# A seventh pair by seven products, its weights streamed in a pinned order

## The chip, the cores and the metric

The kernel runs on one core of a Trainium2 chip. The metric is device time in microseconds (us) of one execution, the median over the runs of a kernel. A core has TensorE (PE in the profile; its weight loads are PEld), VectorE (DVE), ScalarE (ACT), GpSimd (POOL) and SyncE (SP), each with its own instruction queue, and 16 DMA engines that move data between the device memory (HBM, "dram" in the names) and the on-chip memory. Matmuls write accumulators called banks; the program has eight.

## The reference

Two layers of a decoder trunk on x of 512 tokens by 1024 features, in float32. Each layer is an FFN, a mixer (a gated recurrence beside a spatial gate), and another FFN, each followed by a layer norm:

```python
def swiglu(x, w13, w2):
    a, b = jnp.split(x @ w13, 2, axis=-1)
    return (jax.nn.silu(a) * b) @ w2

for l in range(DEPTH):                       # DEPTH = 2
    x = layer_norm(ALPHA * x + 0.5 * swiglu(x, ffn1_w13[l], ffn1_w2[l]), ...)
    x = layer_norm(ALPHA * x + mixer(x, ...), ...)
    x = layer_norm(ALPHA * x + 0.5 * swiglu(x, ffn2_w13[l], ffn2_w2[l]), ...)
```

So there are four FFNs. Each has a hidden width of 2816 = 22 blocks of 128; w13 holds 22 blocks for a and 22 for b. The change touches the first multiplication of each FFN (x by w13) and the first microseconds of the program; the second multiplication and the mixer are as they were.

## The kernel before

**Splitting.** Every operand of a matmul is split in two parts of a format that TensorE takes: hi, a rounded copy made by ScalarE, and lo, the rest, made by VectorE from source and hi (`split`, L117 to L122). A product then takes three matmuls, hi by hi, hi by lo and lo by hi. A weight block is fetched by SyncE's queue into a tile of the ring "raw" (four buffers), then split into two tiles of the ring "w" (ten buffers, so five weights). Other rings are "rs" (two buffers), "sa" (three) and the slots "h" (33).

**Plain blocks.** The hidden blocks are taken in eleven pairs (k, k + 11). A plain block j is `pair_of` with two calls of `proj`: 24 matmuls of 512 columns for a and 24 for b (L147), then `glu`: silu on ScalarE and a product on VectorE (L593, L594). A plain pair is two such blocks.

**Seven products.** Six of the eleven pairs are instead done as a 2 by 2 block multiplication with seven products in place of eight (`seven_pair`). The weights of a pair are four quarters: a, the upper halves of the two a blocks; c, their lower halves; b and d, the same of the two b blocks, chosen by column and row. From the quarters VectorE forms sums (t13, t2 and one more), so that there are seven weights of 128 x 1024, each split into hi and lo. The tokens' side has its own sums s1 to s4, made once per FFN (`x_sums`). Each product is 24 matmuls of 256 columns (L548) into one of the banks A, B, C, E; ScalarE and VectorE then combine the banks (L557 to L572). A, C and E are used twice in a pair: the second product adds on top of the first, so it waits until the first value has been read.

**The order within an FFN.** Three pairs in front by plain blocks (pairs 8, 9, 10), then six by seven products (0 to 5), then two behind by plain blocks (6, 7). Then `Seven.run` does the second multiplication, by the same scheme; for it `weight_sums`, `activation_sums` (for each pair, four operations and two splits on VectorE and two copies on ScalarE, L330 to L336) and `sums_in_dram` (additions done by DMAs in GpSimd's queue) prepare operands. The activation sums of nine pairs are issued between the four plain blocks behind.

**What sets the order on an engine.** The program is written as one stream, and a planner orders each engine's queue by the readiness that it computes. Side work (`Flow`) is put into the stream when a written clock passes its due time. `tc.keep_in_program_order` ties one instruction behind the instruction of the same engine that was written just before it. Before the change it is used on the rounded copies of two weights (c and d) in each pair and on the DMAs of `sums_in_dram`. On an engine, instructions start in the order of its queue.

**The weights of a pair before.** `weights_of_pair` fetches the quarters into two tiles of "raw" and two of "rs" (for the first pair into slots, two blocks ahead), splits five of the seven weights into the ring "w" and two into slots, and is issued ahead of the pair's products. The program starts with `first_block`, which puts six matmuls on a tile of zeros ahead of the first real one.

Of the kernel before, what the change touches and what calls it, by code (L numbers as in the profile page):

```python
# [40 lines left out]
NF = DFF // P  # L41
# [42 lines left out]
def trunk(ctx: ExitStack, tc, x_in, xt_in, w13, w2, w_in, w_br, w_out, ln_g, ln_b, lb_in, hgn, sgg, sgb, sgws,  # L84
          sgbs, masks, tril_in, ident_in, out):
    nc = tc.nc
    V, S, G, PE = nc.vector, nc.scalar, nc.gpsimd, nc.tensor
# [3 lines left out]
    wk = ctx.enter_context(tc.tile_pool(name="wk", bufs=1))  # L91
# [11 lines left out]
    def slot(name, dtype=F32):  # L103
        return big.tile([P, 2, 512], dtype, tag="h", name=name, bufs=NS)
# [10 lines left out]
    xh, xl = [None] * 4, [None] * 4  # L115


    def split(hi, lo, src, pinned=False):
        act = S.activation(hi, src, AF.Copy)  # L119
        if pinned:  # L120
            tc.keep_in_program_order(act)
        V.tensor_tensor(lo, src, hi.bitcast(F32), op=ALU.subtract)  # L122

    def weights(src, name, early=False):

# [10 lines left out]
    NW = 10  # L136
    NS, NRAW, NSA = 33, 4, 3
# [46 lines left out]
    H = slice(0, 512), slice(512, 1024)  # L184
# [75 lines left out]
    NH2 = NF // 2  # L260

    class Seven:
# [51 lines left out]
        def activation_sums(self, k):  # L314

            r = self.r[k]
            x = wk.tile([P, 2, 256], F32, tag="sa", name="s12", bufs=NSA)
            if k >= self.KEPT:
                hi, lo = (quads(f"t{c}{k}", F32R) for c in "hl")
                parts = hi[:, 0], lo[:, 0], hi[:, 1:3], lo[:, 1:3]  # L320
            elif self.last is None:
                hi, lo = (quads(f"t{c}{k}", F32R) for c in "hl")
                self.last = hi, lo
                parts = hi[:, 0], lo[:, 0], hi[:, 1:3], lo[:, 1:3]
            else:
# [4 lines left out]
            V.tensor_tensor(x[:, 0], r[:, 2], r[:, 3], op=ALU.subtract)  # L330
            V.tensor_tensor(x[:, 1], r[:, 0], x[:, 0], op=ALU.subtract)
            split(parts[0], parts[1], r[:, 0])
            V.tensor_tensor(r[:, 2], r[:, 0], r[:, 2], op=ALU.subtract)
            V.tensor_tensor(r[:, 0], r[:, 1], x[:, 1], op=ALU.subtract)
# [152 lines left out]
            s[c] = hi, lo  # L487
        return s

    def raw_cd(w13_of, k, early=False):  # L490

        if early:
            rc, rd = slot(f"rc{k}"), slot(f"rd{k}")
        else:
            rc, rd = (wk.tile([P, 2, 512], F32, tag="rs", name=f"r{c}{k}", bufs=2) for c in "cd")
        for z, j in enumerate((k, k + NH2)):
            nc.sync.dma_start(rd[:, z], w13_of(NF + j)[:, H[0]])
            nc.sync.dma_start(rc[:, z], w13_of(j)[:, H[1]])
        return rc, rd

    def weights_of_pair(w13_of, k, rcd=None):

        js = (k, k + NH2)
        ra = [wk.tile([P, 2, 512], F32, tag="raw", name=f"r_p{j}", bufs=NRAW) for j in js]
        rc, rd = rcd or raw_cd(w13_of, k)
        t13 = [slot(f"t13{j}") for j in js]
        t2 = slot(f"t2{k}")
        for z, j in enumerate(js):
            wa, wb = w13_of(j), w13_of(NF + j)
            nc.sync.dma_start(ra[z][:, 0], wa[:, H[0]])  # L510
            nc.sync.dma_start(ra[z][:, 1], wb[:, H[1]])

        def parts(raw, name, early=False):
            hi, lo = ((slot(f"{v}_{name}", F32R) if early else
                       wk.tile([P, 2, 512], F32R, tag="w", name=f"{v}_{name}", bufs=NW)) for v in "hl")
            split(hi, lo, raw, early)
            return [(hi[:, z], lo[:, z]) for z in range(2)]

        p = [parts(ra[z], f"p{j}") for z, j in enumerate(js)]
        for z in range(2):  # L520
            V.tensor_tensor(t13[z], ra[z], rd[:, z:z + 1].broadcast_to([P, 2, 512]), op=ALU.add)
            V.tensor_tensor(t2[:, z], ra[z][:, 0], t13[z][:, 1], op=ALU.add)  # L522
        w2 = parts(t2, f"t2{k}")
        wt = [parts(t13[z], f"t{j}") for z, j in enumerate(js)]
        w21 = parts(rc, f"c{k}", True)
        V.tensor_tensor(rc, rc, t2, op=ALU.add)
        w4 = parts(rc, f"d{k}", True)
        return p, wt, w2, w21, w4

    def seven_pair(seven, s, k, w):  # L530

        p, wt, w2, w21, w4 = w
        half = slice(0, 256), slice(256, 512)
        movs = {"A11": lambda m: (xh[m // 2][:, m % 2, half[0]], xl[m // 2][:, m % 2, half[0]]),
                "A12": lambda m: (xh[2 + m // 2][:, m % 2, half[0]], xl[2 + m // 2][:, m % 2, half[0]]),
                "A22": lambda m: (xh[2 + m // 2][:, m % 2, half[1]], xl[2 + m // 2][:, m % 2, half[1]])}
        for c in s:
            movs[c] = lambda m, c=c: (s[c][0][:, m], s[c][1][:, m])

        def product(ps, units, c, first=True):  # L540
            for z in range(2):
                hi, lo = units[z]
                for m in range(4):
                    ms = slice(m * P, (m + 1) * P)
                    mh, ml = movs[c](m)
                    for i, (a, v) in enumerate(((hi, mh), (hi, ml), (lo, mh))):
                        start = first and z == 0 and m == 0 and i == 0
                        PE.matmul(ps[:, half[z]], a[:, ms], v, start=start, stop=(m == 3 and i == 2),  # L548
                                  skip_group_check=not (first and z == 0))
# [6 lines left out]
        product(A, [p[0][0], p[1][0]], "A11")  # L556
        S.activation(upper, A, AF.Copy)  # L557
        product(B, w2, "s2")
        V.tensor_tensor(upper, upper, B, op=ALU.subtract)
        product(C, [wt[0][0], wt[1][0]], "s1")  # L560
        V.tensor_tensor(b1, C, upper, op=ALU.subtract)
        product(E, [wt[0][1], wt[1][1]], "s3")
        V.tensor_tensor(b1, b1, E, op=ALU.subtract)
        product(A, w21, "A12", False)
        S.activation(lower, A, AF.Silu)
        product(C, [p[0][1], p[1][1]], "s4", False)
        V.tensor_tensor(b0, C, upper, op=ALU.subtract)
        V.tensor_tensor(lower, lower, b0, op=ALU.mult)
        product(E, w4, "A22", False)
        V.tensor_tensor(upper, E, upper, op=ALU.add)  # L570
        S.activation(upper, upper, AF.Silu)
        V.tensor_tensor(upper, upper, b1, op=ALU.mult)  # L572

    S_PAIRS = 6

    def ffn(l, i, last=False, first_of_all=False):
        seven = Seven(lambda k: w2[l, i, k])
# [22 lines left out]
        sums = iter(range(NH2))  # L600
# [25 lines left out]
        for z, j in enumerate(js[2:]):  # L626
            args = blocks(j)
            if z == 3:
                w = weights_of_pair(w13_of, by_seven[0], rcd)
            plain(j, args)  # L630
            if z == 0:
                s = x_sums()
            if z == 1:
                rcd = raw_cd(w13_of, by_seven[0], True)
            if z == 0:
                seven.weight_sums(next(sums))
            if z == 1:
                seven.activation_sums(front[1])
        in_dram = flow.add(seven.sums_in_dram(list(sums)))
        for k in by_seven:  # L640
            seven_pair(seven, s, k, w if k == by_seven[0] else weights_of_pair(w13_of, k))
        due = [front[2:] + by_seven[:2], by_seven[2:5], by_seven[5:] + behind[:1], behind[1:]]
# [361 lines left out]
    def first_block(wa, wb):  # L1004
# [2 lines left out]
        zero = wk.tile([P, T], F32, tag="sa", name="zero", bufs=NSA)  # L1007
        V.memset(zero[:, 0:P], 0.0)
        idle = bank("idle")
        for _ in range(6):  # L1010
            PE.matmul(idle[:, 0:P], zero[:, 0:P], zero[:, 0:P], start=True, stop=True)
        rw = [wk.tile([P, D], F32, tag="raw", name=f"r_{c}0", bufs=NRAW) for c in "ab"]
        w = [[wk.tile([P, D], F32R, tag="w", name=f"{c}_{v}0", bufs=NW) for c in "hl"] for v in "ab"]
# [137 lines left out]
```

## Time and profile before

| | |
|---|---|
| median of 3 runs | 2078.19 us (2078.13 to 2081.96) |
| the profiled execution, its own time | 2075.15 us |
| its span in the profile | 2073.4 us |
| busy: TensorE, its weight loads, VectorE, ScalarE, GpSimd | 2058.6, 1814.0, 1465.6, 871.3, 284.7 us |
| stage of six pairs by seven products, second FFN | 764.1 to 885.1 us |
| four plain blocks behind it | 885.1 to 928.7 us |

Times in the profile are counted from the first instruction. A row of the timeline reads: start, duration, engine, line, operation, output and inputs by tile names, sizes, count, and in brackets the idle time of the engine ahead of it with what ended it. In rows of groups the mean duration of one is in nanoseconds. A row of DMA issues ends with the median time from issue to landing; "SPq" is SyncE's queue. The rows of waits give total, count and longest, in us.

### The profile page before, as it was taken

What the parts mean: (1) busy time and instruction counts of PE and PEld (TensorE: products, weight loads), DVE (VectorE), ACT (ScalarE), POOL (GpSimd) and SP (SyncE); (2) the same over time, 40 slices, a digit from 0 to 9 for tenths busy, and PEclk for the clock granted to TensorE, in tenths of its full rate; (3) what the DMA queues carried; (4) which work ended last, traced back from release to release, by engine and by line L of the source; (5) the groups of instructions that cost most, each with busy time, mean ns of one, the idle gap of its engine ahead of it and who ended that gap; (6) DMA issues with size and microseconds to landing.
All of it is one profiled execution on the core that took longest, in us unless ns stands there. A gap on an engine that the chain in (4) does not pass through costs nothing.

```text
span 2073.4 us, 30387 instructions
## 1 busy us (share of the span) xinstructions
PE 2058.6 (99%) x11764; PEld 1814.0 (87%) x11764; DVE 1465.6 (71%) x2285; ACT 871.3 (42%) x1219; POOL 284.7 (14%) x424
## 2 busy tenths in 40 slices
PE   9999999999999999999999999999999999999998
PEld 7999888888888989988899998888888888899886
DVE  7986878943535788777778878779444357987776
ACT  4443555234322434446534445542343224444453
POOL 1222002001000222210112220020010002122001
PEclk9999999999999999999999999999999999999999
DMA  8788677122243578867768886861222436788674
GB/s 300 226 236 205 194 267 250 42 82 82 82 156 98 205 222 218 210 172 275 238 219 244 219 216 194 275 209 52 82 90 84 143 97 237 218 217 218 178 264 141
DMA packets 142849, 381.27 MB, mean 184 GB/s; under 512 B 16624, under 2 KB 16880, under 8 KB 142704
## 3 DMA queue, kind: packets, MB, share of 16 engines
q1 hardware_dynamic: 100368, 258.13, 37.3%
q0 software_dynamic: 42336, 121.20, 22.7%
q8 instruction: 92, 1.51, 0.3%
q14 instruction: 53, 0.43, 0.1%
HBM read 344.66 MB, written 101.71 MB: 215 GB/s over the span
## 4 chain that ended last, share of the span: by engine, by line
PE 96%; DMA 2%; DVE 1%; ACT 1%; issue 0%; POOL 0%; SPq 0%; POOLq 0%; DVEq 0%; ACTq 0%
PE pa L147 9%; PE pb L147 9%; PE z L147 8%; PE fC L548 7%; PE fE L548 7%; PE fA L548 7%; PE pA L363 6%; PE pC L363 6%; PE y L229 4%; PE y L147 4%; PE fB L548 3%; PE pB L363 3%; PE pE L363 3%; PE pF L363 3%; PE q L147 2%; PE f L147 2%
## 5 line engine op out<-in xcount | busy, mean ns | idle before, releaser
L122 DVE TENSOR_TENSOR l_b<-r_b,h_b 128x1024 fp32r<-128x1024 f32 (+1 forms) x85 | 102.5, 1210 | 54.3 <-ACT h_b L119 53.8
L288 POOL DMA_DIRECT2D t<-in_w_dram x128 | 106.5, 885 | 215.5 <-DMA t<-in_w_dram 102.7
L147 PE MATMUL pa<-xh,l_a 128*128 128x512 f32 (+1 forms) x360 | 130.0, 361 | 1.0 <-DVE l_a L122 1.0
L147 PE MATMUL pa<-xl,h_a 128*128 128x512 f32 (+1 forms) x360 | 130.4, 362 | 0.5 <-DVE xl L122 0.5
L147 PE MATMUL pb<-xh,h_b 128*128 128x512 f32 (+1 forms) x360 | 130.3, 362 | 0.0
L147 PE MATMUL pa<-xh,h_a 128*128 128x512 f32 (+1 forms) x360 | 130.3, 362 | 0.0
L147 PE MATMUL pb<-xh,l_b 128*128 128x512 f32 (+1 forms) x360 | 129.9, 361 | 0.0
L147 PE MATMUL pb<-xl,h_b 128*128 128x512 f32 (+1 forms) x360 | 129.8, 361 | 0.0
L119 ACT ACTIVATE h_b<-r_b 128x1024 fp32r<-128x1024 f32 (+1 forms) x85 | 89.0, 1047 | 91.4 <-PE pa L147 34.1
L122 DVE TENSOR_TENSOR l_t<-t,h_t 128x1024 fp32r<-128x1024 f32 x72 | 87.3, 1222 | 42.1 <-ACT h_t L119 42.1
L119 ACT ACTIVATE h_t<-t 128x1024 fp32r<-128x1024 f32 x72 | 75.4, 1058 | 67.5 <-DVE t L522 49.1
L147 PE MATMUL z<-xh,h_z 128*128 128x512 f32 x256 | 102.6, 401 | 0.0
L147 PE MATMUL z<-xh,l_z 128*128 128x512 f32 x256 | 99.8, 390 | 0.0
L147 PE MATMUL z<-xl,h_z 128*128 128x512 f32 x256 | 99.8, 390 | 0.0
L122 DVE TENSOR_TENSOR l_z<-r_z,h_z 128x1024 fp32r<-128x1024 f32 x32 | 39.2, 1225 | 72.5 <-ACT h_z L119 72.4
L119 ACT ACTIVATE h_p<-r_p 128x1024 fp32r<-128x1024 f32 x48 | 50.4, 1058 | 69.5 <-PE fE L548 48.9
L147 PEld LDWEIGHTS pa<-xh,l_a 128*128 128x128 f32 x360 | 67.8, 188 | 11.7 <-DVE l_a L122 1.4
L147 PEld LDWEIGHTS pa<-xl,h_a 128*128 128x128 f32 x360 | 67.9, 189 | 11.4 <-DVE xl L122 1.2
L229 PE MATMUL y<-h_wo,yt 128*128 128x512 f32 x256 | 77.3, 392 | 0.0
L147 PEld LDWEIGHTS pa<-xh,h_a 128*128 128x128 f32 x360 | 67.9, 189 | 10.5 <-ACT xh L119 0.3
L147 PEld LDWEIGHTS pb<-xh,l_b 128*128 128x128 f32 x360 | 67.9, 189 | 10.4
L147 PEld LDWEIGHTS pb<-xl,h_b 128*128 128x128 f32 x360 | 67.9, 189 | 10.3
(363 smaller groups left out, 6704.2 us busy)
## 6 DMA issues: line engine op xcount, KB each, us to landing
t<-in_w_dram POOLq DMA_DIRECT2D x64, 512.0 KB, 9.1
r_p<-in_w_dram SPq DMA_DIRECT2D x96, 256.0 KB, 7.6
r_c<-in_w_dram SPq DMA_DIRECT2D x44, 512.0 KB, 5.8
r_d<-t SPq DMA_DIRECT2D x88, 256.0 KB, 4.2
r_a<-in_w_dram SPq DMA_DIRECT2D x39, 512.0 KB, 5.3
r_b<-in_w_dram SPq DMA_DIRECT2D x39, 512.0 KB, 5.5
t<-t POOLq DMA_DIRECT2D x76, 256.0 KB, 4.0
t<-in_w_dram POOLq DMA_DIRECT2D x64, 256.0 KB, 5.6
```

Source lines behind the costliest of these rows:

```text
L119: act = S.activation(hi, src, AF.Copy)
L122: V.tensor_tensor(lo, src, hi.bitcast(F32), op=ALU.subtract)
L147: PE.matmul(ps[:, n0:n0 + n], a[:, cs], m[:, n0:n0 + n], start=(i == 0), stop=(i == 3 * nk - 1))
L229: PE.matmul(ys[t][q], a[:, ts], m[:, q * 512:(q + 1) * 512], start=(k == 0 and i == 0), stop=(k == nk - 1 and i == 2))
L288: tc.keep_in_program_order(nc.gpsimd.dma_start(*of(k), **kw))
L363: PE.matmul(ps[tt], a[:, ts], m, start=(start and k == 0 and z == 0), stop=(stop and k == NH2 - 1 and z == 2), skip_group_check=not start)
L548: PE.matmul(ps[:, half[z]], a[:, ms], v, start=start, stop=(m == 3 and i == 2), skip_group_check=not (first and z == 0))
```

## The change

Seven pairs (0 to 6) go by seven products and one (7) stays plain behind them. A class `PairWeights` fetches the four quarters into a, b and d in the ring "raw" and c in "rs"; the sum t13's part t3 = d + b has the other buffer of "rs", and the sums b + a, a + t3 and later c + a overwrite the quarters. All seven weights of a pair are split into the ring "w". The weights of the next pair are written between the products of the running one, at fixed places, and while `pinned` is set each ScalarE and VectorE instruction of the stage is tied behind the one written before it. The activation sums of pairs 10, 0, 1 and 2 are written behind the seven-product pairs 0 to 3, in the same order; those of pairs 3 to 7 stay between the plain blocks. Ten matmuls on zeros stand ahead of the first real one.

```diff
+    pinned = [False]
+    def pin(ins):
+        if pinned[0]:
+            tc.keep_in_program_order(ins)
+    def split(hi, lo, src):
+        pin(S.activation(hi, src, AF.Copy))
+        pin(V.tensor_tensor(lo, src, hi.bitcast(F32), op=ALU.subtract))
...
+    class PairWeights:
+        def __init__(self, w13_of, k):
+            self.w13_of, self.k, self.w = w13_of, k, {}
+            self.a, self.b, self.d = (self.raw(c, "raw", NRAW) for c in "abd")
+            self.t3 = self.raw("t", "rs", 2)
+            self.load(self.a, 0, 0)
+            self.load(self.b, NF, 0)
+            self.load(self.d, NF, 1)
+        def raw(self, c, tag, n):
+            return wk.tile([P, 2, 512], F32, tag=tag, name=f"r{c}_{self.k}", bufs=n)
+        def load(self, to, col, row):
+            for z, j in enumerate((self.k, self.k + NH2)):
+                nc.sync.dma_start(to[:, z], self.w13_of(col + j)[:, H[row]])
+        def load_last(self):
+            self.c = self.raw("c", "rs", 2)
+            self.load(self.c, 0, 1)
+        def parts(self, p):
+            src = {1: "a", 6: "a", 5: "b", 7: "t3", 2: "c", 3: "d", 4: "c"}[p]
+            hi, lo = (wk.tile([P, 2, 512], F32R, tag="w", name=f"{v}_p{p}_{self.k}", bufs=NW) for v in "hl")
+            split(hi, lo, getattr(self, src))
+            self.w[p] = hi, lo
+        def sums(self):
+            for to, u, v in ((self.t3, self.d, self.b), (self.b, self.a, self.b), (self.a, self.a, self.t3)):
+                pin(V.tensor_tensor(to, u, v, op=ALU.add))
+        def last_sum(self):
+            pin(V.tensor_tensor(self.c, self.a, self.c, op=ALU.add))
...
+        pw.parts(2)
+        pw.last_sum()
+        if next_of is not None:
+            nx = next_of()
+        product(A, w[1], "A11")
+        pin(S.activation(upper, A, AF.Copy))
+        pw.parts(3)
+        product(B, w[6], "s2")
+        pin(V.tensor_tensor(upper, upper, B, op=ALU.subtract))
+        pw.parts(4)
+        if nx:
+            nx.load_last()
+        product(C, w[5], "s1")
+        pin(V.tensor_tensor(b1, C, upper, op=ALU.subtract))
+        if nx:
+            nx.parts(1)
+        product(E, w[7], "s3")
+        pin(V.tensor_tensor(b1, b1, E, op=ALU.subtract))
+        if nx:
+            nx.sums()
+            nx.parts(6)
+        product(A, w[2], "A12", False)
+        pin(S.activation(lower, A, AF.Silu))
+        if nx:
+            nx.parts(5)
+        product(C, w[3], "s4", False)
+        pin(V.tensor_tensor(b0, C, upper, op=ALU.subtract))
+        pin(V.tensor_tensor(lower, lower, b0, op=ALU.mult))
+        if nx:
+            nx.parts(7)
+        product(E, w[4], "A22", False)
+        pin(V.tensor_tensor(upper, E, upper, op=ALU.add))
+        pin(S.activation(upper, upper, AF.Silu))
+        pin(V.tensor_tensor(upper, upper, b1, op=ALU.mult))
+        for v in due:
+            seven.activation_sums(v)
+        return nx
-    S_PAIRS = 6
+    S_PAIRS = 7
...
             if z == 3:
-                w = weights_of_pair(w13_of, by_seven[0], rcd)
+                pinned[0] = True
+                pw = PairWeights(w13_of, by_seven[0])
+                pw.load_last()
+                pw.parts(1)
+                pw.sums()
+                for p in (6, 5, 7):
+                    pw.parts(p)
+                pinned[0] = False
...
+        pinned[0] = True
         for k in by_seven:
+            pw = seven_pair(seven, s, k, pw, (lambda: PairWeights(w13_of, k + 1)) if k < by_seven[-1] else None,
+                            ([front[2]], by_seven[0:1], by_seven[1:2], by_seven[2:3], [], [], [])[k])
+        pinned[0] = False
+        due = [by_seven[3:6], by_seven[6:] + behind]
...
-        for _ in range(6):
+        for _ in range(10):
             PE.matmul(idle[:, 0:P], zero[:, 0:P], zero[:, 0:P], start=True, stop=True)
```

More of the change, by code (lines that the diff above doesn't have):

```diff
@@ L115, in trunk @@
     xh, xl = [None] * 4, [None] * 4
[L118 to L122, printed above, removed]
+    pinned = [False]
[5 more added lines that the diff above has]
+        pin(V.tensor_tensor(lo, src, hi.bitcast(F32), op=ALU.subtract))
     def weights(src, name, early=False):
@@ L488, in x_sums @@
         return s
[L490 to L528, printed above, removed]
@@ L533, in seven_pair @@
+    def seven_pair(seven, s, k, pw, next_of, due):
+        w, nx = pw.w, None
         half = slice(0, 256), slice(256, 512)
@@ L541, in product @@
             for z in range(2):
-                hi, lo = units[z]
+                hi, lo = units[0][:, z], units[1][:, z]
                 for m in range(4):
@@ L555, in seven_pair @@
         b0, b1 = (wk.tile([P, T], F32, tag="sa", name=f"b{c}", bufs=NSA) for c in "01")
[L556 to L572, printed above, removed]
-    S_PAIRS = 6
+        pw.parts(2)
[36 more added lines that the diff above has]
+    S_PAIRS = 7
     def ffn(l, i, last=False, first_of_all=False):
```

14 lines of the change are left out of this document (4 added, 10 removed).

## The prediction

> **What bounds the kernel now.** I read the page's first part, then the stages in the view of stretches, then the chain of waits and who waits on TensorE, then the order of VectorE in one seven-product stage.
>
> ```profile
> span 2073.4 us, 30387 instructions
> PE 2058.6 (99%) x11764; PEld 1814.0 (87%) x11764; DVE 1465.6 (71%) x2285; ACT 871.3 (42%) x1219; POOL 284.7 (14%) x424
> ```
>
> TensorE works for 2058.6 of 2073.4 us. So either a change takes matmul time away, or it makes TensorE wait. The stretches are those of the seven-product stage and of the plain blocks behind it, in the second FFN (the others agree within 0.4 us of VectorE):
>
> ```profile
> core 0: us, PE busy (x) PEld busy (x) DVE busy (x) ACT busy (x) POOL busy (x), PEclk, DMA share, GB/s
> 764.10:885.10 121.00, 121.00 (x1010) 121.00 (x1009) 99.39 (x111) 53.72 (x60) 27.77 (x40) 1.00 0.86 217
> 885.10:928.70 43.60, 43.60 (x194) 36.07 (x193) 30.41 (x62) 17.29 (x30) 5.55 (x8) 1.00 0.62 167
> ```
>
> The stage of six pairs takes 121.0 us without a gap on TensorE, while VectorE works 99.4 us in it (16.6 a pair) and the 16 DMA engines are 0.86 busy. The four plain blocks behind it have more air on both: 30.4 of 43.6 us, and 0.62. The chain of waits in time order and TensorE's list of waits:
>
> ```profile
> 77.82 2.88 PE fB L548 x24
> 80.70 2.88 PE fC L548 x24
> ...
> 195.90 5.47 PE pa L147 x24
> 201.37 5.44 PE pb L147 x24
> ```
>
> ```profile
> PE pa L1041 <- ACT xh L119: 1.4, 1, 1.4
> PE idle L1011 <- DVE zero L1008: 1.1, 1, 1.1
> PE pa L147 <- DVE l_a L122: 1.0, 1, 1.0
> PE pb L1041 <- ACT h_b L119: 0.7, 1, 0.7
> ```
>
> A product is 24 matmuls in 2.88 us; a plain block is 5.44 + 5.44. All listed waits lie in the first 65 us. VectorE's pace inside the stage:
>
> ```profile
> 766.25 1.22 DVE L122 TENSOR_TENSOR l_c<-rc,h_c 128x1024 fp32r<-128x1024 f32 x1
> 767.51 1.22 DVE L526 TENSOR_TENSOR rc<-rc,t 128x1024 f32<-128x1024 f32 x1
> 769.86 1.23 DVE L122 TENSOR_TENSOR l_d<-rc,h_d 128x1024 fp32r<-128x1024 f32 x1 [1.12 <-ACT h_d L119]
> 771.00 0.68 DVE L559 TENSOR_TENSOR r<-r,fB 128x512 f32<-128x512 f32 x1
> 771.60 1.22 DVE L122 TENSOR_TENSOR l_p<-r_p,h_p 128x1024 fp32r<-128x1024 f32 x1
> 772.73 1.22 DVE L521 TENSOR_TENSOR t<-r_p,rd 128x1024 f32<-128x1024 f32 x1
> 773.87 0.68 DVE L561 TENSOR_TENSOR b<-fC,r 128x512 f32<-128x512 f32 x1
> ```
>
> From start to start a full operation (128x1024) takes 1.14 us and a half one (128x512) 0.60; 1.26 where the second overwrites what the first reads (766.25 to 767.51). A sum whose rounded copy is its own next operand costs VectorE 1.12 us of waiting on ScalarE. Today the stage interleaves sums and splits of several weights, and ten of the fourteen hi/lo tiles of a pair go through the w ring and four into other slots, so these waits cost TensorE nothing.
>
> **The change part by part.**
>
> *Matmuls.* One pair per FFN goes from two plain blocks, 4 x 5.44 = 21.76 us, to seven products, 7 x 2.88 = 20.16. That is 1.60 us each, 6.4 us over four FFNs.
>
> *Ten matmuls on zeros instead of six.*
>
> ```profile
> 1.07 2.93 PE L1011 MATMUL idle<-zero 128*128 128x128 f32 x12 [1.07 <-DVE zero L1008]
> 5.44 0.79 PE L1041 MATMUL pa<-xh,h_a 128*128 128x512 f32 x1 [1.44 <-ACT xh L119]
> 6.96 0.80 PE L1041 MATMUL pb<-xh,h_b 128*128 128x512 f32 x1 [0.73 <-ACT h_b L119]
> 7.55 0.63 PE L1041 MATMUL pa<-xl,h_a 128*128 128x512 f32 x1
> ...
> 9.26 0.63 PE L1041 MATMUL pa<-xh,h_a 128*128 128x512 f32 x1
> ```
>
> Six show as 12 records in 2.93 us, so four more add at most 2.0 us and end near 6.0; the second real matmul waits until 6.96 anyway. Between 7.55 and 9.26 four matmuls start 0.43 us apart, later ones 0.23 apart. The most that full speed could save on the seven matmuls from 6.96 on is 7 x 0.20 = 1.4 us; the worst is the 2.0 us of the extra zeros. Behind both stands the wait of 1.0 us on l_a that ends at 64.22, whose chain does not pass through these matmuls:
>
> ```profile
> 33.26 6.44 DMA rb_w<-in_w_dram
> ...
> 62.95 1.23 DVE l_a L122
> 64.18 0.04 issue
> 64.22 5.29 PE pa L147 x22
> ```
>
> An earlier TensorE only waits longer there. I take 0 (bounds -1.4 and +1.0, the extra zeros' 2.0 less what that wait swallows).
>
> *VectorE's work per pair.* Old: ten full operations and nine half ones. New: seven splits, three sums and the last sum, eleven full, and seven evictions, 11 x 1.14 + 7 x 0.60 = 16.7 us; the same. ScalarE keeps seven copies and three evictions, some 9 us of 20.16, and costs nothing of itself.
>
> *The activation sums moved in.* Four of nine (for the pairs front[2], 0, 1, 2) are now issued behind pairs 0 to 3, in the pinned order:
>
> ```profile
> 903.14 0.42 DVE L331 TENSOR_TENSOR s<-r,s 128x256 f32<-128x256 f32 x1
> ...
> 905.42 0.42 DVE L331 TENSOR_TENSOR s<-r,s 128x256 f32<-128x256 f32 x1
> ```
>
> Six operations from one L331 to the next, 2.28 us. With them VectorE has 19.0 us of work in 20.16. The five that stay behind fit: 5 x 2.28 + 2 x (2 x 1.14 + 0.60) = 17.2 us in the 21.76 of the two last blocks, and pair 6 has no successor, which leaves VectorE 11 us free. I cost that at nothing; without that cover it would be those 17.2 less whatever of the 21.76 is gone.
>
> *The order itself.* Every ScalarE and VectorE instruction of the stage is now tied to the one traced before it. So each wait on VectorE holds everything behind it, evictions too. I follow one pair in program order, from the eviction of its predecessor's last product (start to start; L568 to L572 stands for the round trip through Silu):
>
> ```profile
> 885.27 0.69 DVE L570 TENSOR_TENSOR r<-fE,r 128x512 f32<-128x512 f32 x1
> 886.65 0.69 DVE L572 TENSOR_TENSOR r<-r,b 128x512 f32<-128x512 f32 x1 [0.70 <-ACT r L571]
> 887.26 0.75 DVE L330 TENSOR_TENSOR s<-r 128x256 f32<-128x256 f32 x2
> ```
>
> (i) upper+E, Silu, times b1: 1.99. (ii) activation sums: 2.28. (iii) split 2, then the last sum over the operand just read, to its end: 1.26 + 1.22 = 2.48. (iv) split 3, subtract B, split 4, b1 from C, split 1 of the next pair, subtract E: 3 x 1.14 + 3 x 0.60 = 5.2. (v) three sums: 3.42. (vi) wait for the copy of the last of them 1.12, split 6 1.14. (vii) split 5 with 0.3 of waiting (ScalarE does the Silu of the fifth product, 0.6, between two copies): 1.44. (viii) b0 and its product, the second needing the first: 1.29; split 7: 1.14. Sum: 1.99 + 2.28 + 2.48 + 5.2 + 3.42 + 2.26 + 1.44 + 2.43 = **21.5 us** with activation sums, 19.2 without. TensorE's period is 20.16.
>
> *The load of the next pair.* A pair holds three raw tiles (a, b, d) of a ring of four. At the time its loads are traced, only the fourth and b's have been let go; the third must wait for the last sum of the running pair, (iii), the last reader of a. With tiles given as they come free that is d, and the first of the three sums (v) needs d. Such a load is two DMAs of 256 KB; the sync queue issues them right when the buffer is free:
>
> ```profile
> 775.07 1.22 DVE L521 TENSOR_TENSOR t<-r_p,rd 128x1024 f32<-128x1024 f32 x1
> ```
>
> ```profile
> 776.31 0.80 SPq L497 DMA_DIRECT2D rd<-in_w_dram  x2
> ```
>
> ```profile
> rd<-in_w_dram SPq DMA_DIRECT2D x48, 256.0 KB, 7.2
> rc<-in_w_dram SPq DMA_DIRECT2D x48, 256.0 KB, 6.8
> ```
>
> ```profile
> DMA to landing us min/median/max: 2.5/6.8/11.4
> ```
>
> The last row is rc's, which like the new d is issued as two alone. I take its 6.8 us (bounds 2.5 and 11.4). If (iv)'s 5.2 us are replaced by this wait, the ring last sum, d, sums, splits, evictions, last sum takes 16.3 + 6.8 = **23.1 us** with activation sums and 20.8 without. Behind the waiting sum stand the splits of parts 6, 5 and 7 and the evictions b0 and the last two; TensorE waits for all of them. Behind d's DMAs in the sync queue stand the next a and the next c, both with a pair's time to spare. POOL's queue, with its sums in DRAM, is neither passed nor moved; its traffic is what the loads share the DMA engines with.
>
> The Trainium skill (DMA: Bandwidth & Descriptors, "Anatomy of one DMA — SWDGE (gpsimd) path") gives one transfer about 2.0 us plus its bytes at 436 GB/s, fitted on the other DMA path; for 512 KB that is an estimate of 3.2 us. By it d would be in time and the sum would be that of the first rival below; the median of 6.8 us at a DMA share of 0.86 says otherwise.
>
> *What TensorE feels.*
>
> ```profile
> L548 PE MATMUL fA<-xh,h_p 128*128 128x256 f32 x192 | 54.3, 283 | 0.0
> ```
>
> A product's last matmul ends 0.16 us after its 0.12 us slot. So subtracting E in pair 0 can start at 4 x 2.88 + 0.2 = 11.7 us of the pair; (v) to (viii) follow, so the eviction at its end starts at 11.7 + 0.6 + 3.42 + 2.26 + 1.44 + 2.43 = 21.9, a lag of 1.7 over 20.16. Each pair behind activation sums (1 to 4) adds 23.1 - 20.16 = 2.9, pair 5 adds 0.6: 1.7 + 11.6 + 0.6 = 13.9 us at the end. The room: product six of a pair reuses C and must wait for b1, which ends 1.99 + 2.28 + 2.48 + 1.14 + 0.60 + 1.14 + 0.68 = 10.3 us after the late eviction began, against the sixth product's start at 14.4. Room: 4.1 us. The w ring gives the same to within 0.3: split 6 must end 23.3 us after the pair's start and ends 6.75 + 6.8 + 3.42 + 1.12 + 1.22 = 19.3 after the eviction. So TensorE loses 13.9 - 4.1 = **9.8 us** an FFN, 39 in all. The d of pair 0, whose quarters were fetched two blocks ahead before and are not now, is a further 0 to 1.8 each (its buffer comes free some 11 us ahead of the stage, its first use is 3 us into it); I take 0.
>
> *Sum.* -6.4 + 39 + 0 = +33 us on the profiled execution's 2075.15: 2108. The median of the runs shown is 3.0 over it, so **2111 us**.
>
> **Rivals.**
>
> *d lands in time.* If loads take 5.2 us or less, the loop is 21.5 and the lag grows by 1.3 in four pairs and shrinks afterwards: 1.7 + 5.4 - 4.1 = 3.0 an FFN, 12 in all, -6.4 + 12 = +5.6, so 2084. For it: some loads land in 2.5 us, and the new ones are spread more evenly. Against it: the median.
>
> *The gain is kept.* If the lag never passes 4.1, TensorE stays gapless and the time is 2078.2 - 6.4 = 2072. This is decided where a pair's loop, waits included, stays at 20.16 + (4.1 - 1.7) / 4 = 20.8 us or below. For it: the plain work is 19.0 us, the stage before shows no stall on TensorE, and 1.12, 0.3 and 0.70 of waiting are all that must be added, which misses by 0.7 only. Against it: the wait for d must then vanish too.
>
> *Two loads behind the last sum.* If the ring of raw tiles is given out in turn, b of the next pair gets a's buffer, and d queues behind it: four DMAs, 8.3 us or more to the last (6.8 + two issues of 0.4 + some queueing). The loop is 24.6 + and the lag 1.7 + 4 x 4.4 + 2.1 = 21.4, the loss 17.3 an FFN: -6.4 + 69 = +63, so 2141.
>
> *The ten matmuls alone act* (the pins bind nothing, each engine's order as the planner has it): as the gain kept, at 2071 to 2072; within that rival's chance.
>
> **How the numbers follow.** The forecast 0.57, own range 2088 (loads of 5.5 us) to 2136 (8.0 us); d in time 0.17; gain kept 0.19; two loads 0.07. What a measurement here tells from no change is about 0.2%, 4.2 us. Faster holds the gain kept and nothing else: 0.19. "Same" is half of d in time: 0.09. Slower is the rest: 0.72. The range of 8 in 10 reaches from just under the gain kept, 2071, to 2136.
>
> **What would show it.** Right: the stage grows from 20.16 to about 22 us a pair with gaps on TensorE before the sixth and the second product, released by VectorE's b1 and by split 6; VectorE idle before the sum t3, released by the DMA of d; gaps in pairs 2 to 5, none in pair 6. The first rival: same gaps, but VectorE idle only before splits 6 and 5 and after Silu. Gain kept: seven pairs in 141.1 us with TensorE gapless. I am wrong in the working if d's DMAs are not issued right behind the last sum, or if VectorE's order in the stage is not program order.

## The result, and the profile after

The changed kernel takes 2131.76 us (median of five runs, 2128.79 to 2137.18) against 2078.13 us (five runs, 2077.58 to 2081.96): a ratio of 1.0261, 95% interval 1.024 to 1.0281. It is slower by 54 us. The profiled execution of after took 2130.46 us. The first part of its page:

```profile
span 2128.6 us, 31183 instructions
PE 2075.2 (97%) x12060; PEld 1833.6 (86%) x12060; DVE 1520.1 (71%) x2309; ACT 877.1 (41%) x1235; POOL 284.9 (13%) x424
```

The span grew by 55.2 us. The four stages of seven pairs hold all of that. The view of stretches of after, one row for each FFN's stage (columns as in the prediction's: length, busy time of each engine, granted clock, DMA share, GB/s):

```profile
core 0: us, PE busy (x) PEld busy (x) DVE busy (x) ACT busy (x) POOL busy (x), PEclk, DMA share, GB/s
74.40:233.00 158.60, 147.28 (x1177) 143.54 (x1176) 133.35 (x152) 65.91 (x81) 33.15 (x46) 0.99 0.81 201
780.00:936.20 156.20, 147.51 (x1177) 144.77 (x1176) 132.68 (x152) 65.90 (x81) 33.15 (x46) 0.98 0.81 203
1133.50:1287.10 153.60, 145.36 (x1177) 143.23 (x1177) 133.19 (x152) 65.84 (x81) 34.16 (x47) 0.99 0.80 207
1834.70:1991.80 157.10, 146.12 (x1177) 142.13 (x1176) 133.18 (x153) 65.86 (x81) 33.25 (x47) 1.00 0.80 202
```

Seven pairs without a gap are 7 x 20.16 = 141.1 us. The stages are 17.5, 15.1, 12.5 and 16.0 us longer, 61.0 in all before rounding; less the 6.4 us of matmuls saved, that is +54.6, the growth of the span to within 0.6. TensorE's list of waits says where it stood (total, count, longest):

```profile
PE fC L549 <- DVE b L570: 18.8, 17, 1.9
PE fB L549 <- DVE l_p L127: 8.1, 12, 0.8
PE fB L549 <- ACT h_p L126: 5.3, 6, 1.3
PE fA L549 <- ACT h_p L126: 3.0, 7, 0.5
PE fA L549 <- DVE l_p L127: 1.9, 7, 0.3
PE fC L549 <- ACT r L579: 1.3, 2, 0.7
```

The first row is the sixth product, which reuses bank C and waits for b1. The next two are the second product, which waits for split 6. TensorE waits little at a time and often, as an engine does that follows a loop slightly slower than itself. That loop is VectorE's. Its order from one sum t3 (L525, `rt`) onward, second FFN, in the timeline of after:

```profile
797.83 1.23 DVE L525 TENSOR_TENSOR rt<-rd,rb 128x1024 f32<-128x1024 f32 x1 [2.76 <-DMA rd<-in_w_dram]
...
813.59 1.23 DVE L528 TENSOR_TENSOR rc<-ra,rc 128x1024 f32<-128x1024 f32 x1
819.34 0.68 DVE L574 TENSOR_TENSOR b<-b,fE 128x512 f32<-128x512 f32 x1
820.44 1.23 DVE L525 TENSOR_TENSOR rt<-rd,rb 128x1024 f32<-128x1024 f32 x1 [0.42 <-DMA rd<-in_w_dram]
821.70 1.23 DVE L525 TENSOR_TENSOR rb<-ra,rb 128x1024 f32<-128x1024 f32 x1
822.96 1.22 DVE L525 TENSOR_TENSOR ra<-ra,rt 128x1024 f32<-128x1024 f32 x1
825.39 1.23 DVE L127 TENSOR_TENSOR l_p<-ra,h_p 128x1024 fp32r<-128x1024 f32 x1 [1.21 <-ACT h_p L126]
...
842.55 1.22 DVE L525 TENSOR_TENSOR rt<-rd,rb 128x1024 f32<-128x1024 f32 x1
866.09 1.23 DVE L525 TENSOR_TENSOR rt<-rd,rb 128x1024 f32<-128x1024 f32 x1 [1.36 <-DMA rd<-in_w_dram]
888.20 1.22 DVE L525 TENSOR_TENSOR rt<-rd,rb 128x1024 f32<-128x1024 f32 x1
911.40 1.23 DVE L525 TENSOR_TENSOR rt<-rd,rb 128x1024 f32<-128x1024 f32 x1 [3.20 <-DMA rd<-in_w_dram]
```

The sync queue of after between the two events of that loop, and the times from issue to landing and the waits in the view of d's tile (`rd`, all four stages):

```profile
814.85 0.80 SPq L511 DMA_DIRECT2D rd<-in_w_dram  x2
```

```profile
who waited for it (us, times):
  DVE rt L525: 37.0, 16
...
DMA to landing us min/median/max: 2.7/6.1/9.8
```

Here is the ring in one place. The last sum of the running pair ends at 813.59 + 1.23 = 814.82, d of the next pair is issued at 814.85, it lands 5.5 us later, and t3 starts at 820.44. Where t3 waits for nothing, the loop is 842.55 - 820.44 = 22.11 us, still longer than TensorE's 20.16. Where it waits, the loop reaches 23 and more.

### The profile page after: what moved, and what is told of

Its sections match the earlier page's. It is cut to its first block, busy times and chain, and to the rows that moved or that the text cites. A ratio compares the mean times of both kernels' runs of the same rounds, so it can differ in the third digit from the quotient of the medians.

```text
span 2128.6 us, 31183 instructions
## 1 busy us (share of the span) xinstructions
PE 2075.2 (97%) x12060; PEld 1833.6 (86%) x12060; DVE 1520.1 (71%) x2309; ACT 877.1 (41%) x1235; POOL 284.9 (13%) x424
## 4 chain that ended last, share of the span: by engine, by line
PE 30%; DVE 8%; issue 6%; DMA 4%; ACT 2%; POOL 1%; SPq 0%; POOLq 0%; DVEq 0%; ACTq 0%
PE z L152 4%; PE pA L368 3%; PE pC L368 3%; DMA rd<-in_w_dram 3%; DVE l_p L127 2%; PE y L152 2%; PE pB L368 1%; PE pF L368 1%; PE pE L368 1%; PE y L234 1%; PE fC L549 1%; PE q L152 1%; PE f L152 1%; PE fE L549 1%; PE i L738 1%
## 5 line engine op out<-in xcount | busy, mean ns | idle before, releaser
L126 ACT ACTIVATE h_p<-ra 128x1024 fp32r<-128x1024 f32 x56 | 58.8, 1050 | 226.3 <-DVE ra L525 211.4
L549 PE MATMUL fA<-xh,h_p 128*128 128x256 f32 x448 | 128.3, 286 | 3.7 <-ACT h_p L126 3.0
L549 PE MATMUL fA<-xh,l_p 128*128 128x256 f32 x448 | 127.7, 285 | 1.9 <-DVE l_p L127 1.9
L549 PE MATMUL fA<-xl,h_p 128*128 128x256 f32 x448 | 126.8, 283 | 0.0
L152 PE MATMUL pa<-xh,l_a 128*128 128x512 f32 (+1 forms) x296 | 105.0, 355 | 0.0
L127 DVE TENSOR_TENSOR l_p<-ra,h_p 128x1024 fp32r<-128x1024 f32 x56 | 68.3, 1219 | 33.7 <-ACT h_p L126 33.7
L549 PEld LDWEIGHTS fA<-xh,h_p 128*128 128x128 f32 x448 | 85.9, 192 | 6.5 <-ACT h_p L126 4.4
L549 PEld LDWEIGHTS fA<-xh,l_p 128*128 128x128 f32 x448 | 85.9, 192 | 3.6 <-DVE l_p L127 3.5
L549 PEld LDWEIGHTS fA<-xl,h_p 128*128 128x128 f32 x448 | 85.9, 192 | 0.2
L549 PE MATMUL fC<-xs4h,h_p 128*128 128x256 f32 x224 | 66.2, 296 | 20.1 <-DVE b L570 18.8
```

What stands on the lines that cost most here:

```text
L126: pin(S.activation(hi, src, AF.Copy))
L127: pin(V.tensor_tensor(lo, src, hi.bitcast(F32), op=ALU.subtract))
L152: PE.matmul(ps[:, n0:n0 + n], a[:, cs], m[:, n0:n0 + n], start=(i == 0), stop=(i == 3 * nk - 1))
```

## The experiments

Unless it is said otherwise, each kernel is the changed kernel with the edit shown. "Excess" is a stage's length over 141.1 us, in the order of the four FFNs. The loop is VectorE's, from one sum t3 to the next. Comparisons are with the kernel before on the same chip. Where no interval is given, there was one execution.

**1. The four activation sums back behind the stage.**

```diff
-                            ([front[2]], by_seven[0:1], by_seven[1:2], by_seven[2:3], [], [], [])[k])
+                            ([], [], [], [], [], [], [])[k])
-        due = [by_seven[3:6], by_seven[6:] + behind]
+        due = [front[2:] + by_seven[:4], by_seven[4:] + behind]
```

> All nine activation sums go back behind the seven products (four pairs' sums at the first of the two plain blocks, with front[2], five at the second); nothing else changes. Theory (a pinned ring of the load of d and VectorE's own operations sets the pace): without the 2.3 to 2.5 us of sums the ring is 14.4 + 6.2 = 20.6 us instead of 22.8, so nearly all stalls of the pairs go and only the late first load (8.7 us in all) and a few long loads stay: 2080 to 2095, with up to 18 us more if the sums now overfill the plain blocks. Rival (the load of d alone sets the pace, the sums only fill its waits): 2120 or above.

Measured: 2133.63 us (2130.23 to 2142.48), ratio 1.0272 (1.0247 to 1.0297). Nothing was gained. The view of d's tile of this kernel:

```profile
who waited for it (us, times):
  DVE rt L525: 72.0, 21
...
DMA to landing us min/median/max: 3.4/7.5/11.4
```

The 2.5 us a pair that VectorE saved went into the wait for d: 72.0 us in place of 37.0, and the landing moved from a median of 6.1 to 7.5 us (one execution each; this one, at 2142.48 us, was the longest of four). The excess is 17.5, 17.9, 14.3 and 10.4, in all 60.1 against 61.0. In addition the second multiplication now waits some 9 us for its operands, which come later. The load looked like the bound by itself, and it had become longer while VectorE had less to do. Experiments 9 to 11 look at what lengthens it.

**2. A fifth raw buffer.** The next d no longer waits for the last sum. A slot of "h" is given up for the space.

```diff
-    NS, NRAW, NSA = 33, 4, 3
+    NS, NRAW, NSA = 32, 5, 3
```

> A fifth buffer for the raw tiles (one slot fewer of the h ring pays for it): the third quarter of the next pair, d, no longer waits for the last sum of the running pair, nor for the last plain block ahead of the stage. Theory: no wait on d, no late first pair; VectorE's own loop of 22.1 us stays, growing 1.9 us in four pairs against a room of 4.1, so 5 to 6 us an FFN plus 1 to 2 of halved matmul rate remain: 2095 to 2105. Rival (the load alone): 2070 to 2075. Rival (VectorE's order alone, loads hidden in it anyway): 2120 or above.

Measured: 2083.40 us (2082.51 to 2086.28), ratio 1.0023 (1.0011 to 1.0034): 48 us less than the changed kernel. TensorE's waits of this kernel:

```profile
PE fC L549 <- DVE b L570: 6.8, 10, 0.9
PE fA L549 <- ACT h_p L126: 3.3, 8, 0.8
```

The stretch of the second FFN's stage, and d's landing:

```profile
765.44:910.50 145.06, 142.46 (x1177) 141.42 (x1176) 127.65 (x148) 63.21 (x78) 34.00 (x47) 1.00 0.83 215
```

```profile
DMA to landing us min/median/max: 2.6/4.0/9.3
```

The second product's wait for split 6 is gone, nothing waits for d as a load before t3, and every stage has the same excess of 3.95 us. The loop is 22.10 or 22.11 us throughout. So the wait for d carried about three quarters of the 61 us, and the loop without it costs 4 us an FFN, less than expected.

**3. Both.** Fifth buffer, and the sums behind the stage.

> Both at once: five raw buffers and no activation sums in the stage. Theory: the loop is 19.6 us with no load in it, the stage is gapless at 141.1 us, and the kernel is 6.4 us faster than before, 2070 to 2075, if the two plain blocks hold the nine sums; up to 2090 if they do not. Rival (seven products at this place cost more than the plain blocks for another reason): over 2085 with gaps in the stage.

Measured: 2075.68 us (2074.86 to 2077.77), ratio 0.9991 (0.9981 to 1.0). All four stages take 141.11 us, without a gap. Of the 6.4 us of matmuls only a part is left, since the second multiplication again waits for the late sums (its banks B and A wait 5.1 and 2.4 us in the profile).

**4. The pins off, four buffers as in the change.**

```diff
-                pinned[0] = True
+                pinned[0] = False
...
-        pinned[0] = True
+        pinned[0] = False
```

> The instructions of the stage are not tied to one another, so the planner orders ScalarE and VectorE; buffers, loads and sums as in the change. Theory: d still waits for the last sum, and the planner works with its own idea of when loads land, so stalls stay but the 1.2 and 0.7 us holes may be filled: 2090 to 2130. Rival (the pins alone are the cause): 2070 to 2080.

Measured: 2152.41 us (2149.54 to 2161.29), ratio 1.0363 (1.0339 to 1.0388), outside what any theory expected. TensorE's waits:

```profile
PE fC L549 <- DVE b L570: 30.8, 8, 6.6
PE fE L549 <- DVE b L574: 20.4, 10, 3.5
```

The waits are fewer and longer, up to 6.6 us, and the excess is 21.8, 20.6, 21.2 and 17.1. With four buffers the pinned order is better than the planner's by some 20 us. The pins are not the cause of the loss.

**5. Fifth buffer, and split 5 ahead of split 6.** Part 5 is the second of the three sums, part 6 the third; the third sum runs while ScalarE rounds the second.

```diff
             nx.sums()
-            nx.parts(6)
+            nx.parts(5)
...
         if nx:
-            nx.parts(5)
+            nx.parts(6)
```

> Fifth raw buffer and the activation sums where the change puts them, but split 5 (whose source is ready one sum earlier) is issued ahead of split 6. Theory: VectorE's hole of 1.2 us ahead of split 6 and that of 0.2 us ahead of split 5 close, the loop falls from 22.1 to 20.7 us, the lag to 1.7 + 4 x 0.6 = 4.1 us, just inside the room, so the stage is gapless or nearly (at most 0.5 us an FFN): 2071 to 2075, 8 to 12 us under the fifth buffer alone. Rival (the room is smaller than 4.1, or the hole only moves): 2078 to 2083.

Measured: 2067.41 us (2066.62 to 2067.91), ratio 0.995 (0.9937 to 0.9962). All stages are 141.11 us. VectorE's timeline of this kernel around the three sums:

```profile
793.58 1.22 DVE L525 TENSOR_TENSOR rt<-rd,rb 128x1024 f32<-128x1024 f32 x1
794.83 1.23 DVE L525 TENSOR_TENSOR rb<-ra,rb 128x1024 f32<-128x1024 f32 x1
796.09 1.23 DVE L525 TENSOR_TENSOR ra<-ra,rt 128x1024 f32<-128x1024 f32 x1
797.31 1.23 DVE L127 TENSOR_TENSOR l_p<-rb,h_p 128x1024 fp32r<-128x1024 f32 x1
798.74 1.22 DVE L127 TENSOR_TENSOR l_p<-ra,h_p 128x1024 fp32r<-128x1024 f32 x1 [0.21 <-ACT h_p L126]
```

The 1.21 us of idling ahead of the first split are gone, since its rounded copy was made during the third sum. The loop falls from 22.1 to 20.9 us: still over 20.16, but now within the room for the few pairs that carry activation sums (18.7 us without them).

**6. As 5, and split 7's rest put into the round trip through Silu.**

```diff
         if nx:
-            nx.parts(7)
+            nx.high_of_7()      # the rounded copy of part 7, on ScalarE
         product(E, w[4], "A22", False)
         pin(V.tensor_tensor(upper, E, upper, op=ALU.add))
         pin(S.activation(upper, upper, AF.Silu))
+        if nx:
+            nx.low_of_7()       # its rest, on VectorE
         pin(V.tensor_tensor(upper, upper, b1, op=ALU.mult))
```

> As the one before, and split 7 of the next pair stands between the last sum of a pair and its last product, in the 0.7 us in which VectorE waits for Silu. Theory: loop 20.0 us, below TensorE's 20.16; stage gapless, 141.1 us; the whole gain of 6.4 us shows, 2070 to 2073. Rival (something outside the stage takes it back, as the 4 us in the run with the sums behind): 2075 to 2078.

Measured: 2067.09 us (2065.24 to 2070.06), ratio 0.995 (0.9937 to 0.9962). That is no difference from 5 that can be told: the stage was gapless already. The stretch of the second FFN's stage and the whole of TensorE's waits in this kernel, to hold against the rows of after:

```profile
core 0: us, PE busy (x) PEld busy (x) DVE busy (x) ACT busy (x) POOL busy (x), PEclk, DMA share, GB/s
759.60:900.70 141.10, 141.10 (x1178) 141.10 (x1177) 128.68 (x148) 64.14 (x78) 33.30 (x47) 1.00 0.85 225
```

```profile
PE idle L1050 <- DVE zero L1047: 1.1, 1, 1.1
PE pa L152 <- DVE l_a L127: 0.2, 1, 0.2
```

The profiled span is 2063.5 us, 9.9 below before's 2073.4: 6.4 are the matmuls, 2.6 come from a stage that starts at 72.2 in place of 74.8 us, and 0.9 is not placed. The start of the first stage moves from profile to profile (with ten zeros 72.2 us in 6, 73.2 in 8, 74.4 in 3; with six 74.5 in 7), so the 2.6 is a reading of one execution, not a shown gain.

**7. As 6, with six matmuls on zeros in place of ten.**

```diff
-        for _ in range(10):
+        for _ in range(6):
```

> The one before with six matmuls on zeros instead of ten. Theory: no difference that shows, within 1 us, since the next binding wait (l_a near 64 us) does not pass through the first matmuls. Rival (the ten warm TensorE up): slower by 1 to 2 us.

Measured: 2068.54 us (2066.1 to 2069.77), ratio 0.9954 (0.9941 to 0.9966), an interval that covers most of 6's. The median is 1.5 us above that of 6 and within the spread of both, so neither the theory nor the rival's 1 to 2 us is excluded. The program's first matmuls in the timeline of after, and below them those of 6:

```profile
1.07 3.94 PE L1040 MATMUL idle<-zero 128*128 128x128 f32 x20 [1.07 <-DVE zero L1037]
...
7.71 0.80 PE L1070 MATMUL pb<-xh,h_b 128*128 128x512 f32 x1 [1.62 <-ACT h_b L126]
...
10.86 0.45 PE L1070 MATMUL pa<-xl,h_a 128*128 128x512 f32 x1
```

```profile
1.07 4.63 PE L1050 MATMUL idle<-zero 128*128 128x128 f32 x20 [1.07 <-DVE zero L1047]
...
6.74 0.39 PE L1080 MATMUL pa<-xh,l_a 128*128 128x512 f32 x1
```

Ten zeros show as 20 records. In after they end at 5.0 us, waits of 0.57 and 1.62 us follow, and the real matmuls start 0.43 us apart until 10.86; before, it was until 9.69. In 6 no wait stands between zeros and real matmuls, and from 6.74 on these start some 0.23 us apart. In 7, with six zeros and waits of 0.90 and 1.41 us, they do so from 11.93 on. The waits are for the rounded copies of the first operands, and they differ from execution to execution; how much of the earlier full rate in 6 is due to the zeros is not shown.

**8. Fifth buffer, pins off.** The edits of 2 and 4.

> Fifth raw buffer, no pins, all else as in the change. It tells what the hand-made order is worth when loads are in time. Theory (the planner lets evictions wait, as the 51 us of waits on b1 in the run without pins show): 2085 to 2120, slower than the same with pins (2083). Rival (the pins are the harm, the planner fills the holes): 2071 to 2080.

Measured: 2067.49 us (2066.71 to 2068.38), ratio 0.9952 (0.9937 to 0.9967); all stages 141.11 us. The expectation fell: with five buffers the planner's own order is gapless, and 16 us better than the pinned order of the change. So the order of the change helps only while loads come late; with loads in time it costs the 4 us an FFN of experiment 2, which the swap of experiment 5 avoids. Kernels 5, 6, 7 and 8 are all some 10 to 11 us faster than before, and nothing here tells them apart.

**9. GpSimd's additions written behind the stage.** For 9, 10 and 11 only the stage is read, since the second multiplication then waits for what the additions prepare. They have four buffers and the pinned order of the change.

```diff
-        in_dram = flow.add(seven.sums_in_dram(list(sums)))
         pinned[0] = True
...
         pinned[0] = False
+        in_dram = flow.add(seven.sums_in_dram(list(sums)))
```

> The changed kernel with GpSimd's additions in DRAM started behind the seven-product stage instead of at its beginning; four raw buffers, pins and sums as in the change. Only the stage is to be read, since the second multiplication then waits for the additions. Theory (loads of d are long because they share the DMA engines with these additions): d lands 3 to 4.5 us after its issue, there is no wait on it, and the stage has the excess of the fifth buffer plus the late first pair, 4 to 6.5 us an FFN. Rival (a load of two times 256 KB takes its 6 us anyway): the excess stays at 12 to 17 us.

Measured: 2107.48 us, excess 10.3, 9.5, 9.3 and 10.5. The edit did only half of what it was to do: GpSimd's queue let the additions in some 28 us into the stage all the same. Until then d landed 3.3 to 4.4 us after its issue, afterwards 6.0 on average; and the first pair, whose d had landed 9 to 10 us after issue in the changed kernel and landed after 6.1 to 6.6 here, lost nothing. Inconclusive as it stood, so it was made to bind:

**10. The additions held until the last pair's result.** A small GpSimd operation that reads pair 6's result stands ahead of them in the queue.

```diff
         pinned[0] = False
+        late = small("late")
+        tc.keep_in_program_order(G.tensor_scalar(late, seven.r[6][:, 0, 0:1], 1.0, 0.0, op0=ALU.mult, op1=ALU.add))
+        in_dram = flow.add(seven.sums_in_dram(list(sums)))
```

> GpSimd's additions in DRAM are held back by one GpSimd instruction that reads the last pair's result, so that none of them runs in the seven-product stage (the planner had let them in after some 28 us in the run before). Four raw buffers, pins, activation sums as in the change. Only the stage is to be read, since the second multiplication then waits for the additions. Theory: d lands 3.3 to 4.4 us after issue as in the free part of the run before, no wait on it, loop 22.1 us, excess 4 to 6 us an FFN. Rival (a fourth buffer's load is slow in itself): waits on d stay, excess 9 us or more.

**11. The same with the activation sums behind the stage**, that is, 10 and 1.

> The one before, and all nine activation sums behind the stage. In the first run this alone saved nothing in the stage, because the loads took 7.8 us instead of 6.2. Theory: with the additions away the loads take 3.3 to 4.4 us, so the ring is 14.4 + 4.4 = 18.8 us, under 20.16, and the stage is gapless or within 2 us an FFN (the first pair). Rival (something else in the four-buffer order holds the pace): excess over 5 us.

Measured: the whole programs take 2411.73 and 2399.31 us, since the second multiplication waits some 280 us for its operands. The stage is another matter. The stretch of the second FFN's stage and d's landing in 10:

```profile
851.05:996.30 145.25, 142.48 (x1178) 141.45 (x1177) 130.38 (x150) 65.72 (x81) 1.08 (x2) 1.00 0.32 111
```

```profile
who waited for it (us, times):
  DVE rt L525: 3.5, 1
...
DMA to landing us min/median/max: 2.5/3.2/6.4
```

and the stretch in 11:

```profile
845.45:986.50 141.05, 141.05 (x1177) 141.05 (x1176) 121.63 (x125) 62.18 (x72) 1.04 (x1) 1.00 0.34 113
```

With GpSimd quiet (1.1 us busy in place of 33) and the DMA share down from 0.81 to 0.32, the median landing of one of d's DMAs is 3.2 us. The wait in the list is that of a first pair and costs TensorE nothing. The excess is 3.94, 4.10, 3.93 and 3.96, the loop 22.10: the numbers of the fifth buffer, reached with four. And in 11 the sums behind the stage give what they did not give in 1, four stages of 141.11 us. So the load is long because the additions run beside it, and the ring of four buffers is what carries that length into VectorE's order. What load and additions contend for, the DMA engines or the memory behind them, no run tells apart. Nor does the DMA share alone set the length: in 2 the additions run too, the share is 0.83, and d's median is 4.0 us. There d is issued some 9 us ahead of the next a, in the changed kernel 1.1 us ahead of it. In 1 the loads grew by as much as the pairs' work shrank: the 16 behind the pairs that had the activation sums ahead of them take 8.0 us on average in place of 5.5. Why is not shown: the four stages together are as long as those of the changed kernel, and the DMA share in them (0.76 to 0.82) is about the same.

## Why the prediction was right, and where it was off

**The result**, 2131.76, lies in the range, near its upper end; the forecast of 2111 was 21 us short. The cause forecast is the cause shown: last sum, d's load, the three sums, splits and evictions on one VectorE queue, and TensorE behind it at the sixth and the second product. Experiments 2 and 10 take away one link each, the shared buffer and the load's length, and the excess falls from 61 to 16 us both times.

**The matmuls** (-6.4) hold: gapless stages measure 141.11 for 7 x 20.16. **The ten zeros** (0, bounds -1.4 and +1.0) are not contradicted: experiment 7's 1.5 us is within the spread and can't tell 0 from the bound. **The five activation sums that stay behind** cost nothing, as costed: TensorE's list of waits in after has no row of the second multiplication. Moving all nine behind (experiments 1 and 3) does cost.

**VectorE's own loop** with activation sums was taken as 21.5 us and is 22.1. The order was right; three terms in it were small. The three sums start 1.26 us apart, not 1.14 (+0.36). The wait ahead of split 6 is 1.21, not 1.12. The activation sums of one pair take 2.52 us, not 2.28.

**d's load** was taken as 6.8 us; from the first issue to the last landing the mean of the 24 loads behind a running pair is 6.2, 7.6 for the second pair's, 7.7 for the last pair's and 5.5 for the four between. The loop with both came out at about 22.8 us over the pairs with activation sums, where 23.1 was forecast: two errors of opposite sign. The 6.8 was that of rc, issued alone; the new d has the next a 1.1 us behind it. The Trainium skill (DMA: Bandwidth & Descriptors, "Anatomy of one DMA — SWDGE (gpsimd) path") gave the estimate of 3.2 us for 512 KB. Experiment 10's whole loads of 512 KB behind a running pair take 3.3 to 4.6 us, 3.8 on average, at a DMA share of 0.32, so the estimate is near the shortest of them; its median of 3.2 us is for one of the two DMAs. Beside the additions, at 0.81, the mean of a whole load is 6.2 and the estimate does not hold.

**The loss at TensorE** was to be 39 us in all by lag and room, all of it in pairs 2 to 5. Pair by pair, the 61.0 us are 8.7 in the four pairs 0, 37.9 in pairs 1 to 5, 8.5 in the four pairs 6, and 5.9 at a halved rate (below). So the term meets its size, but that is partly chance: 8.3 of the 37.9 are lost in pair 1, where a lag of 1.7 was to stay inside the room. By the same working the loop of 22.1 alone should cost 1.7 + 4 x 1.94 - 4.1 = 5.4 us an FFN, and experiments 2 and 10 measure 4.0: the room was larger or the lag smaller by 1.4. Pair 5 was to lose a little and loses almost nothing.

**Pair 6** was to have no gap and loses 8.5 us over the four FFNs. Its load took 7.7 us and not 6.8, and the loop in front of it, without activation sums, measures 22.1 to 23.2 us where 20.8 was forecast. Only the last pair's own lack of a successor had been looked at, not the work for it during pair 5.

**The first d late** (0, bounds 0 to 1.8 each) is the first mis-sized term. This d was issued some 11 us ahead of the stage, as counted, but landed only 9.0 to 10.3 us later; VectorE waited 6.4 to 7.7 us for it. The first two products of the stage are longer by 2.6, 1.6, 2.5 and 2.0 us, 8.7 in all. Between d's landing and the end of split 6 lie some 6.3 us of sums, waiting and splitting, so a load of up to some 7.7 us would have cost nothing. Experiment 9, without additions at that moment, loads this d in 6.1 to 6.6 us and loses nothing there. The step that failed is the choice of 0: it priced this load like those inside the stage.

**TensorE's rate after a gap** is a term that the prediction did not have. The view of stretches of after, around one wait of 1.92 us for b1 that ends at 818.43:

```profile
816.50:820.00 3.50, 1.58 (x14) 1.60 (x14) 3.50 (x5) 0.44 (x1) 1.44 (x3) 0.99 0.91 314
820.10:823.40 3.30, 3.30 (x18) 3.30 (x17) 2.89 (x3) 0.00 (x0) 1.30 (x3) 0.51 1.03 195
823.40:826.00 2.60, 2.60 (x24) 2.60 (x24) 1.39 (x2) 1.70 (x3) 0.00 (x0) 1.00 1.02 343
```

After the gap TensorE does a dozen matmuls at full rate, then for 3.3 us the granted clock is 0.51 and matmuls start 0.213 us apart in place of 0.120, then it is 1.00 again. That is 16 matmuls and 1.5 us more. It happens four times in after's stages, 5.9 us in all: twice in pair 6, and not behind every gap of that length (three others of 1.93 or 1.94 us have no such stretch behind them; what tells them apart was not found). The Trainium skill (TensorE: Matmul & The Clock Gate, "Why this matters for your kernels") has it that gaps of more than some 3 us bring the lower rate. Here the lower rate followed one gap of 1.92 us, one of 1.77, and twice two gaps of 0.7 to 0.9 us close together, and the measurement decides.

So the sum of the prediction, mended: -6.4 + 37.9 + 8.7 + 8.5 + 5.9 = +54.6 us, against 55.2 of growth in the span.

**The rivals.** *d lands in time* was worked out as +5.6 us; experiments 2 and 10 are that case, and 2 measures +5.3 us against before. The closeness is in part luck: by stages the loss of 2 is 15.8 us, where 12 was worked out, which would give +9.4. *The gain is kept* is what experiments 5, 6 and 8 show, with the point from which it decides near where it was put: a loop of 20.9 us is gapless, one of 22.1 is not, and 20.8 was named (the first two measured with five buffers). *Two loads behind the last sum* did not happen: the sync queue issues d, then the next a, and only later b and c. *The ten matmuls alone act*, that is, pins that bind nothing, fell with experiment 4, which differs by 20 us.

**What stays open.** Why the planner's order is worse than the pinned one with four buffers was not followed further than its waits for b1. Of the 11 us that the best kernels gain, 6.4 are shown; the rest, seen at the start of the first stage and in places too small to name, is not.

## What to carry to other kernels

In an order written out by hand, look for the load whose buffer is freed by the last reader in the same in-order queue that needs the load next: its whole time from issue to landing then stands in the loop, and one more buffer (here one slot moved from one ring to another) took away three quarters of the loss. Price such a load in the traffic that will run beside it at that moment, at the stage's start too, and do not take it as fixed when the loop changes (experiment 1). Where a summed order passes the bound engine's pace by a us or two a pair, count the small waits behind each dependent operation: with the fifth buffer in, filling one of 1.2 us was enough to keep the gain.

## What the runs showed of the hardware that was not expected

- TensorE's granted clock fell to 0.51 for 3.3 us behind gaps of 1.77 and 1.92 us and, twice, behind two gaps of 0.7 to 0.9 us, starting 1.2 to 1.7 us after the gap; short waits can cost 1.5 us more than they last. Three gaps of 1.93 or 1.94 us had nothing behind them.
- One DMA of a load of 2 x 256 KB lands in 3.2 us (median) at a DMA share of 0.32. Beside GpSimd's additions in DRAM it lands in 6.1 (changed kernel, share 0.81), 7.5 (experiment 1, 0.76 to 0.82) or 4.0 (experiment 2, 0.83). When VectorE's work for a pair was shortened by 2.5 us (experiment 1), the 16 loads concerned grew from 5.5 to 8.0 us.
- Twenty records of matmuls on zeros, from 1.07 to 5.0 us, with waits of 0.57 and 1.62 us behind them, left the first real matmuls 0.43 us apart until 10.86 us. With no wait behind them (experiment 6), these were 0.23 us apart from 6.74 us on.
